# A hybrid encoder layer on one Trainium2 core: four small changes to the start, the first projection, the seam behind it, and the end

## The chip, the cores and the metric

The kernel runs on one core of one Trainium2 chip. The time is the device time of one execution in microseconds (us); the figure given is the median of three runs. A profiled execution of the same program gives the trace and the page of the profile. Of the engines, TensorE (PE) multiplies matrices, with weight loads (PEld) that overlap the products; VectorE (DVE), ScalarE (ACT) and GpSimd (POOL) work on vectors; SyncE (SP) only issues transfers (DMAs), which ScalarE and GpSimd can issue as well.

## The reference, cut to what matters

One layer for 512 tokens of width 2048, all in float32:

```python
def rmsnorm(x, w):
    return x * lax.rsqrt(jnp.mean(x * x, axis=-1, keepdims=True) + NORM_EPS) * w

h = rmsnorm(x, attn_norm_w)
aq, ak, av, gq, gk, gv, gr, glr = split(h @ w_in)
attn = mixture_of_dilations(heads(aq), heads(ak), heads(av), rel_bias_table)  # three windowed patterns
gla_out = ...                       # gated linear attention in both directions, from gq, gk, gv, gr, glr
x = x + concatenate([attn, gla_out]) @ w_out
h = rmsnorm(x, ffn_norm_w)
x = x + (silu(h @ w_gate) * (h @ w_up)) @ w_down     # hidden width 5632
return rmsnorm(x, final_norm_w)
```

The change touches four places of this computation: the first norm's factors at the very start, the projection to `aq` and `ak`, the passage from it to the next projection, and the last rows of the final norm.

## The kernel before, in words

**Precision.** Each float32 operand of a product is split in two: a rounded high part (a cast, mostly on ScalarE) and the remainder (a subtraction on VectorE). A product is then three matmuls: high by high, high by low, low by high.

**Buffers.** SBUF buffers come from lists that are first in, first out: `get` takes the front of the list, `put` appends at its back. `s2` holds buffers of 128x512 (named a in the profile), `s4` buffers of 128x1024 and larger groups (b). A buffer that has been put back early may be taken again at once; the instruction that writes it then waits until its last reader, a DMA too, is done. `ps` are the eight PSUM banks.

**Stages, in order.** (1) The start: `start0` issues the loads of x's first blocks and of the first weights, the norm's weights (`wrow1`, 16x128) are turned into columns with a transpose (L1154) that needs the identity `idn`, and `prep(0)` transposes x's first block (L450), scales it (L455) and so makes the first operand of the first matmul (L346). `spin(n)` issues n matmuls on a buffer of zeros (L1124) that fill TensorE's time. (2) A projection to `av`. (3) The first projection proper, class `Front`: the columns of `aq` and `ak` in 8 units of 256 columns with four pieces of the contraction each. (4) The other projections of `w_in`, run as jobs over a stream of weights `st`; the attention and the gated linear attention run beside them as side work. (5) The product with `w_out`. (6) The gate and up products of the feed-forward layer, class `Feed`: 44 units, of which 42 use the same emptying code as `Front`. (7) The product with `w_down`, and `finish`, which makes the final norm.

**Units of the first projection and of the feed-forward layer.** Their products use sums of blocks (L1399, L1401 add weights; L1412 casts; L1417 subtracts), so that seven products in seven banks replace eight. `products` issues one piece: 28 wide matmuls (L1508) and 28 narrow ones (L1494). After a unit's last piece `evac7` empties the seven banks into five `s2` buffers `t, v, r1, r2, r3` and one `s4` buffer `c`: ScalarE copies (L1534 into `t`, L1535 to L1542 into `r3, r2, r1, c`), VectorE adds and subtracts (lambdas in L1528 and L1529). A `yield` later, VectorE adds `v` to `c`, and GpSimd issues four DMAs that add `r1`, `r2` and twice `r3` into `c` (L1554 to L1557; `b<-a` in the trace). VectorE then scales `c` and it is stored. In `before` the two buffers `t, v` are put back first, and `r1, r2, r3` after the DMAs are issued. In the stage of `Front` the list then holds just these five.

**The stream and the seam.** `st.split(upto)` casts half pieces (L237, ScalarE) and subtracts (L218, VectorE) up to a number, and gives raw buffers back for the next loads. The seam is where the last unit of `Front` ends and the next job begins, with matmul L337; that job's first `split` stands, in program order, behind the last unit's `evac7`.

**The end.** `finish` works through four row blocks of 128 tokens. For the last block and its last 512 columns `last(ys)` forms the products in two halves of 256 columns (L2059), adds them to the residual (L2073), takes the sum of squares with ScalarE (`Square` with a sum), multiplies by the norm's weights (L2078), forms the reciprocal root with `Ln`, `Exp` and one Newton step in small operations (L2081 to L2085 and the lines behind them), scales the four pieces of 512 columns (L2092) and stores them.

The order of the instructions on each engine is that of the program. Engines run on their own and wait for one another through semaphores.

Of the kernel before, what the change touches and what calls it, by code (L numbers as in the profile page):

```python
# [18 lines left out]
AF = mybir.ActivationFunctionType  # L19
OP = mybir.AluOpType  # L20
# [3 lines left out]
P = 128  # L24
D = 2048
# [6 lines left out]
EPS = 1e-6  # L32
# [86 lines left out]
def layer(nc, tc, x, attn_norm_w, w_in, rel_table, gw_f, gb_f, gw_b, gb_b, gla_norm_w, w_out,  # L119
# [7 lines left out]
    with tc.manual_schedule(), \  # L127
# [302 lines left out]

        dve.memset(warm, 0.0)
        xt[0] = [s4.get(F32, [P, 4, 256]) for _ in range(2)]
        act.dma_start(out=wrow1, in_=attn_norm_w[0].rearrange("(r c) -> r c", c=P))
        act.dma_start(out=idn, in_=c_idn)

        rb = {}
        hT = {}
# [74 lines left out]
        def squares(c, t, tiles, ss):  # L512
            junk = s2.get()
            act.activation(junk.t, tiles[t].t, AF.Square, accum_out=ss[:, t * 4 + c:t * 4 + c + 1])
            put(junk)

        sum1, rstd1 = small[:, 16:20], small[:, 20:24]
# [609 lines left out]
        def start0():  # L1127
            tables(EXP_LN)
            spin(5)
            for k in range(4):  # L1130
                first_x(k)
                if k % 2 == 0:
                    pc = st.pieces[k // 2]
                    pc[1] = s4.get()
                    st.held += 1
                    st.n_dma += 1
                for src, dst in pc[0]:
                    sp.dma_start(out=dst(pc[1].t)[:, k % 2:k % 2 + 1], in_=src[:, k % 2:k % 2 + 1])
            for c in range(1, 4):
                xt[c] = [s2.get() for _ in range(4)]  # L1140
            load_x(1, 0, 256)
            st.limit = 3
            st.load()
            load_x(1, 256, 512)
            st.limit = 4
            st.load()
            load_x(2, 0, 512)
            load_x(3, 0, 512)
            for r, w in ((0, ffn_norm_w), (16, gla_norm_w), (24, gb_f), (28, gb_b)):
                n = w[0].shape[0] // P  # L1150
# [3 lines left out]
            pe.transpose(b.t, wrow1, idn[0:16, 0:16])  # L1154
            dve.tensor_copy(wcol[:, 0:16], b.t)
            put(b)
            spin(2)
            prep(0)
            spin(1)

        def between0(i, b):
            if i == 0 and b == 1:
# [260 lines left out]
        class Feed(Blocks):  # L1423
# [100 lines left out]
            def evac7(self, u, banks):  # L1524
# [111 lines left out]
        class Front(Feed):  # L1636
# [24 lines left out]
            def run(self):  # L1661
                banks = {}
                for i, (u, q) in enumerate(self.seq):
# [371 lines left out]
        def finish():  # L2035
# [25 lines left out]
            def last(ys):  # L2061

                t, c = 3, 3
                m, r = scr[0][:, 0:1], scr[1][:, 0:1]
                pre, q = scr[0][:, 1:2], scr[1][:, 1:2]
                sm, sq = sum2[:, t:t + 1], scr[0][:, 2:3]
                junk = s2.get()
                x_ = x1[c][t].t
                for h in range(2):
# [3 lines left out]
                    dve.scalar_tensor_tensor(x_[:, cols], b.t[:, cols], rstd2[:, t:t + 1], x_[:, cols],  # L2073
                                             op0=OP.mult, op1=OP.add)
# [3 lines left out]
                    dve.tensor_tensor(ys[c].t[:, cols], x_[:, cols], wf[c].t[:, cols], op=OP.mult)  # L2078
                    if h == 0:
                        dve.tensor_reduce(sm, ss2[:, 4 * t:4 * t + 4], op=OP.add, axis=mybir.AxisListType.X)  # L2080
                        dve.tensor_scalar(pre, sm, 1.0 / D, EPS, op0=OP.mult, op1=OP.add)  # L2081
                act.activation(q, sq, AF.Ln, scale=1.0 / D, bias=pre)
                act.activation(r, q, AF.Exp, scale=-0.5)
                dve.scalar_tensor_tensor(m, sq, 1.0 / D, pre, op0=OP.mult, op1=OP.add)
                dve.scalar_tensor_tensor(q, r, r, m, op0=OP.mult, op1=OP.mult)  # L2085
                dve.tensor_scalar(q, q, -0.5, 1.5, op0=OP.mult, op1=OP.add)
                rs = rstdf[:, t:t + 1]
                dve.tensor_tensor(rs, r, q, op=OP.mult)
                act.activation(ys[2].t, ys[2].t, AF.Copy, scale=rs)
                for c in (0, 2, 1, 3):  # L2090
                    if c != 2:
                        dve.tensor_scalar(ys[c].t, ys[c].t, rs, None, op0=OP.mult)  # L2092
                    (act if c >= 2 else sp).dma_start(out=out[t * P:(t + 1) * P, c * 512:(c + 1) * 512], in_=ys[c].t)
                put(junk)

            def run():
                for t in range(4):
                    ys = []
                    for c in range(4):
# [8 lines left out]
                        squares(c, t, x1[c], ss2)  # L2108
# [54 lines left out]
```

## Time and profile before

| | |
|---|---|
| median of three runs | 2183.57 us (2182.68 to 2184.25) |
| profiled execution, its time | 2181.53 us |
| its span | 2179.8 us |
| TensorE busy | 2161.3 us, 99%, 12618 matmuls |
| weight loads busy | 1904.2 us, 87% |
| VectorE busy | 1771.2 us, 81% |
| ScalarE busy | 1195.9 us, 55% |
| GpSimd busy | 338.9 us, 16% |
| moved by DMA | 397.81 MB, mean 183 GB/s |
| chain that ended last | PE 89%, issue 6%, DMA 2%, DVE 2%, ACT 1% |

The span goes from the first to the last instruction that the profile shows; the profiled execution's own time is 1.7 us longer. Matmuls are pipelined and their ends are modelled, so a busy TensorE isn't always one at its pace. In a row of the timeline the columns are the start, the duration, engine, line, operation, out<-in, shapes, count, and in brackets the idle time before it and what ended it. A row of the chain of waits has the start, the duration and what ran; a row of the waits has what waited, for what, the sum of the time in us, how often, and the longest. A row of the windows has, behind the length, for each of PE, PEld, DVE, ACT and POOL the busy time and count (PE's sum first), then the granted clock (1.00 is full), the share of DMA time and GB/s.

### The profile page before, as it was taken

What the parts mean: (1) busy time and instruction counts of PE and PEld (TensorE: products, weight loads), DVE (VectorE), ACT (ScalarE), POOL (GpSimd) and SP (SyncE); (2) the same over time, 40 slices, a digit from 0 to 9 for tenths busy, and PEclk for the clock granted to TensorE, in tenths of its full rate; (3) what the DMA queues carried; (4) which work ended last, traced back from release to release, by engine and by line L of the source; (5) the groups of instructions that cost most, each with busy time, mean ns of one, the idle gap of its engine ahead of it and who ended that gap; (6) DMA issues with size and microseconds to landing.
All of it is one profiled execution on the core that took longest, in us unless ns stands there. A gap on an engine that the chain in (4) does not pass through costs nothing.

```text
span 2179.8 us, 34563 instructions
## 1 busy us (share of the span) xinstructions
PE 2161.3 (99%) x12618; PEld 1904.2 (87%) x12618; DVE 1771.2 (81%) x3073; ACT 1195.9 (55%) x2189; POOL 338.9 (16%) x474
## 2 busy tenths in 40 slices
PE   9999999999999999999999999999999999999998
PEld 7888878888888888988888888888888899999986
DVE  5698767776766557899999898998999888898885
ACT  7445456776554335555555555555555655555562
POOL 0011231110011110012212122121221220021300
PEclk9999999999999999999999999999999999999999
DMA  6376774543337873377767777677776975576982
GB/s 201 125 187 173 189 226 141 176 140 111 105 103 270 288 247 107 120 182 177 198 176 183 180 176 196 178 181 182 177 196 176 263 201 182 181 183 157 283 304 78
DMA packets 256856, 397.81 MB, mean 183 GB/s; under 512 B 18925, under 2 KB 154269, under 8 KB 256686
## 3 DMA queue, kind: packets, MB, share of 16 engines
q1 hardware_dynamic: 201262, 272.43, 39.3%
q0 software_dynamic: 54960, 122.58, 24.9%
q8 instruction: 99, 1.62, 0.3%
q14 instruction: 71, 0.58, 0.1%
q10 hardware_dynamic: 464, 0.60, 0.1%
HBM read 285.37 MB, written 64.29 MB: 160 GB/s over the span
## 4 chain that ended last, share of the span: by engine, by line
PE 89%; issue 6%; DMA 2%; DVE 2%; ACT 1%; POOL 0%; ACTq 0%; DVEq 0%; POOLq 0%
PE ps L1508 27%; PE ps L1494 14%; PE ps L346 6%; PE ps L347 6%; PE ps L348 6%; PE ps L1864 5%; PE ps L1865 5%; PE ps L1863 5%; PE ps L339 3%; PE ps L337 3%; PE ps L338 3%; DMA b<-a 2%; PE ps L662 1%; PE ps L1086 1%; PE ps L630 1%
## 5 line engine op out<-in xcount | busy, mean ns | idle before, releaser
L1412 ACT CAST b<-b 128x768 fp32r<-128x768 f32 (+1 forms) x537 | 489.4, 945 | 338.5 <-DVE b L1417 151.2
L1417 DVE TENSOR_TENSOR b<-b,b 128x768 fp32r<-128x768 f32 (+1 forms) x537 | 563.6, 1084 | 32.9 <-ACT b L1412 21.5
L1508 PE MATMUL ps<-b,b 128*128 128x512 f32 x1552 | 451.4, 393 | 0.4 <-ACT b L1412 0.2
L1508 PE MATMUL ps<-a,b 128*128 128x512 f32 x1248 | 366.0, 394 | 3.3 <-DVE b L1528 3.3
L1508 PEld LDWEIGHTS ps<-b,b 128*128 128x128 f32 x1552 | 263.5, 188 | 30.6 <-ACT b L1412 0.7
L1494 PEld LDWEIGHTS ps<-b,b 128*128 128x128 f32 x1552 | 253.1, 190 | 35.8
L1494 PE MATMUL ps<-b,b 128*128 128x256 f32 x1552 | 275.6, 280 | 0.0
L1494 PEld LDWEIGHTS ps<-a,b 128*128 128x128 f32 x1248 | 208.1, 189 | 34.1 <-DVE b L1417 0.5
L1508 PEld LDWEIGHTS ps<-a,b 128*128 128x128 f32 x1248 | 207.2, 189 | 23.3 <-ACT a L1540 4.0
L1494 PE MATMUL ps<-a,b 128*128 128x256 f32 x1248 | 223.8, 281 | 0.0
L1399 DVE TENSOR_TENSOR b<-b 128x512 f32<-128x512 f32 x244 | 167.2, 685 | 17.8 <-DMA b<-in_w_down_dram 7.0
L1864 PE MATMUL ps<-b,b 128*128 128x256 f32 x624 | 176.8, 283 | 0.0
L1863 PE MATMUL ps<-b,b 128*128 128x256 f32 x624 | 176.8, 283 | 0.0
L1865 PE MATMUL ps<-b,b 128*128 128x256 f32 x624 | 176.8, 283 | 0.0
L346 PE MATMUL ps<-b,b 128*128 128x512 f32 x352 | 139.8, 397 | 0.3 <-ACT b L455 0.3
L348 PE MATMUL ps<-b,b 128*128 128x512 f32 x352 | 137.6, 391 | 0.0
L347 PE MATMUL ps<-b,b 128*128 128x512 f32 x352 | 137.5, 391 | 0.0
L1865 PEld LDWEIGHTS ps<-b,b 128*128 128x128 f32 x624 | 119.9, 192 | 0.0
L1863 PEld LDWEIGHTS ps<-b,b 128*128 128x128 f32 x624 | 119.9, 192 | 0.0
L1864 PEld LDWEIGHTS ps<-b,b 128*128 128x128 f32 x624 | 119.9, 192 | 0.0
L218 DVE TENSOR_TENSOR b<-b,b 128x512 fp32r<-128x512 f32 x143 | 95.9, 686 | 26.1 <-ACT b L237 26.0
L1401 DVE TENSOR_TENSOR b<-b,b 128x256 f32<-128x256 f32 x244 | 103.8, 425 | 8.4
(296 smaller groups left out, 4351.7 us busy)
## 6 DMA issues: line engine op xcount, KB each, us to landing
b<-in_w_gate_dram SPq DMA_DIRECT2D x109, 512.0 KB, 3.9
b<-in_w_up_dram SPq DMA_DIRECT2D x88, 512.0 KB, 3.7
b<-in_w_down_dram SPq DMA_DIRECT2D x88, 512.0 KB, 5.9
b<-in_w_in_dram SPq DMA_DIRECT2D x78, 512.0 KB, 4.0
b<-a POOLq DMA_DIRECT2D x150, 256.0 KB, 4.6
b<-in_w_out_dram SPq DMA_DIRECT2D x32, 512.0 KB, 6.6
gd<-b POOLq DMA_DIRECT2D x22, 512.0 KB, 3.9
b<-gd SPq DMA_DIRECT2D x22, 512.0 KB, 5.6
```

The source lines that it names most:

```text
L346: mm(o, xh.t[:, c], wh.t[:, w], start=first and not on, stop=False, skip_group_check=on)
L347: mm(o, xh.t[:, c], wl.t[:, w], start=False, stop=False, skip_group_check=on)
L348: mm(o, xl.t[:, c], wh.t[:, w], start=False, stop=last, skip_group_check=on)
L1399: dve.tensor_tensor(s_[:, :, 0:2], r[:, :, 1:3], r[:, :, 0:1].to_broadcast(shape), op=OP.add)
L1401: dve.tensor_tensor(s_[:, :, 3], s_[:, :, 2], r[:, :, 3], op=OP.add)
L1412: act.copy(o, src)
L1417: dve.tensor_tensor(o, src, h, op=OP.subtract)
L1494: mm(o, wl, xh, start=False, stop=end, skip_group_check=True)
L1508: mm(o.rearrange("p (s t) -> p s t", s=2), wh, x_, start=first and p == 0, stop=False, skip_group_check=True)
L1863: mm(o, xh[:, t], wh, start=first and h == 0, stop=False, skip_group_check=True)
L1864: mm(o, xh[:, t], wl, start=False, stop=False, skip_group_check=True)
L1865: mm(o, xl[:, t], wh, start=False, stop=last, skip_group_check=True)
```

## The change

1. The load of the identity goes to SP's queue, ahead of all its other loads, instead of being second on ScalarE's queue. Of the filling matmuls, one stands before `prep(0)` and two behind it, instead of the reverse.
2. In `evac7`, the five buffers are put back together after the DMAs are issued, in the order `r1, r3, t, r2, v`, instead of `t, v` before and `r1, r2, r3` after.
3. In `Front.run`, before the products of the last piece of the last unit, two half pieces of the next job's weights are split.
4. At the end, for the last block: the sums of squares of its first four groups go to `ss1`, together with a constant for the epsilon that GpSimd writes. ScalarE adds up these five columns, scaled, with a copy. The last 256 columns' squares are summed by VectorE (`tensor_tensor_reduce`) instead of ScalarE. The product of root and correction is no longer formed; VectorE scales all four pieces by both factors, and the stores alternate between the queues of SP and ScalarE.

```diff
         xt[0] = [s4.get(F32, [P, 4, 256]) for _ in range(2)]
+        sp.dma_start(out=idn, in_=c_idn)
         act.dma_start(out=wrow1, in_=attn_norm_w[0].rearrange("(r c) -> r c", c=P))
-        act.dma_start(out=idn, in_=c_idn)
...
+            spin(1)
+            prep(0)
             spin(2)
-            prep(0)
-            spin(1)
...
                 add(c[:, 256:768], c[:, 256:768], v.t)
-                put(t, v)
                 pool.dma_start(out=c[:, 0:512], in_=r1.t, accum_op=OP.add)
                 pool.dma_start(out=c[:, 512:1024], in_=r2.t, accum_op=OP.add)
                 pool.dma_start(out=c[:, 256:768], in_=r3.t, accum_op=OP.add)
                 pool.dma_start(out=c[:, 768:1024], in_=r3.t[:, z], accum_op=OP.add)
-                put(r1, r2, r3)
+                put(r1, r3, t, r2, v)
...
+                    if u == len(self.units) - 1 and q == 3:
+                        st.split(jobs[n_front].first + 2)
                     self.products(i, banks[u])
...
         def load_wf():
+            pool.memset(ss1[:, 4:5], EPS * D)
...
-                    acc = (ss2[:, 4 * t + 3:4 * t + 4], sq)[h]
-                    act.activation(junk.t[:, cols], x_[:, cols], AF.Square, accum_out=acc)
+                    if h == 0:
+                        act.activation(junk.t[:, cols], x_[:, cols], AF.Square, accum_out=ss1[:, 3:4])
+                        act.activation(ss1[:, 8:13], ss1[:, 0:5], AF.Copy, scale=1.0 / D, accum_out=total)
+                        dve.tensor_tensor(ys[c].t[:, cols], x_[:, cols], wf[c].t[:, cols], op=OP.mult)
+                        continue
+                    dve.tensor_tensor_reduce(junk.t[:, cols], x_[:, cols], x_[:, cols], 1.0 / D, 0.0,
+                                             op0=OP.mult, op1=OP.add, accum_out=sq)
+                    act.activation(q, sq, AF.Ln, bias=total)
+                    act.activation(r, q, AF.Exp, scale=-0.5)
+                    dve.tensor_tensor(m, sq, total, op=OP.add)
                     dve.tensor_tensor(ys[c].t[:, cols], x_[:, cols], wf[c].t[:, cols], op=OP.mult)
-                    if h == 0:
-                        dve.tensor_reduce(sm, ss2[:, 4 * t:4 * t + 4], op=OP.add, axis=mybir.AxisListType.X)
-                        dve.tensor_scalar(pre, sm, 1.0 / D, EPS, op0=OP.mult, op1=OP.add)
-                act.activation(q, sq, AF.Ln, scale=1.0 / D, bias=pre)
-                act.activation(r, q, AF.Exp, scale=-0.5)
-                dve.scalar_tensor_tensor(m, sq, 1.0 / D, pre, op0=OP.mult, op1=OP.add)
-                dve.scalar_tensor_tensor(q, r, r, m, op0=OP.mult, op1=OP.mult)
+                dve.scalar_tensor_tensor(q, r, m, r, op0=OP.mult, op1=OP.mult)
                 dve.tensor_scalar(q, q, -0.5, 1.5, op0=OP.mult, op1=OP.add)
-                rs = rstdf[:, t:t + 1]
-                dve.tensor_tensor(rs, r, q, op=OP.mult)
-                act.activation(ys[2].t, ys[2].t, AF.Copy, scale=rs)
-                for c in (0, 2, 1, 3):
-                    if c != 2:
-                        dve.tensor_scalar(ys[c].t, ys[c].t, rs, None, op0=OP.mult)
-                    (act if c >= 2 else sp).dma_start(out=out[t * P:(t + 1) * P, c * 512:(c + 1) * 512], in_=ys[c].t)
+                for c in range(4):
+                    o = ys[c].t
+                    dve.tensor_scalar(o, o, r, q, op0=OP.mult, op1=OP.mult)
+                    (sp, act)[c % 2].dma_start(out=out[t * P:(t + 1) * P, c * 512:(c + 1) * 512], in_=o)
```

More of the change, by code (lines that the diff above doesn't have):

```diff
@@ L510, in squares1, with squares @@
             put(junk)
-        def squares(c, t, tiles, ss):
+        def squares(c, t, tiles, ss, at_=None):
             junk = s2.get()
-            act.activation(junk.t, tiles[t].t, AF.Square, accum_out=ss[:, t * 4 + c:t * 4 + c + 1])
+            m = c + (4 * t if at_ is None else at_)
+            act.activation(junk.t, tiles[t].t, AF.Square, accum_out=ss[:, m:m + 1])
             put(junk)
@@ L2063, in last @@
                 t, c = 3, 3
-                m, r = scr[0][:, 0:1], scr[1][:, 0:1]
-                pre, q = scr[0][:, 1:2], scr[1][:, 1:2]
-                sm, sq = sum2[:, t:t + 1], scr[0][:, 2:3]
+                sq, total = ss1[:, 16:17], ss1[:, 17:18]
+                m, r, q = ss1[:, 18:19], ss1[:, 19:20], ss1[:, 15:16]
                 junk = s2.get()
@@ L2107, in run @@
                         residual(c, t, b)
-                        squares(c, t, x1[c], ss2)
+                        squares(c, t, x1[c], ss2 if t < 3 else ss1[:, 0:4], 0 if t == 3 else 4 * t)
                         if t == 3:
```

## The prediction

> **What bounds the kernel now.** I read first the waits of TensorE over the whole execution, then the busy time by stretch.
>
> ```profile
> PE ps L1508 <- DVE b L1528: 3.5, 5, 1.7
> PE ps L1154 <- DMA idn<-in_c_idn_dram: 1.3, 1, 1.3
> PE ps L337 <- ACT b L237: 1.3, 1, 1.3
> ```
> ```profile
> 20.00:105.00 85.00, 85.00 (x397) 69.01 (x396) 55.19 (x118) 54.44 (x130) 2.79 (x5) 1.00 0.41 135
> 920.00:1720.00 800.00, 800.00 (x4592) 702.64 (x4591) 728.89 (x1128) 440.48 (x742) 155.07 (x184) 1.00 0.72 185
> ```
>
> TensorE is busy 85.00 us of 85 and 800.00 of 800 (first figure behind the stretch's length). So it is the bound, and a gain exists only where it waits or before it starts and after it ends. The three waits are the places that the change aims at; whatever is won there stays won, because nothing idles behind it.
>
> **Part 1, the copies' buffers.** The first projection has units of 28 matmuls a piece and four pieces. At the end of a unit ScalarE and VectorE empty its banks into t, v, r1, r2, r3. The view is ScalarE's timeline; L1534 (into t) marks the end of a unit, L1535 is the first copy into r3.
>
> ```profile
> 161.24 0.37 ACT L1534 COPY a<-ps 128x256 f32<-128x256 f32 x1 [0.54 <-PE ps L1494]
> ...
> 180.74 0.37 ACT L1534 COPY a<-ps 128x256 f32<-128x256 f32 x1
> 185.21 0.37 ACT L1535 COPY a<-ps 128x256 f32<-128x256 f32 x1 [4.10 <-DMA b<-a]
> ...
> 200.76 0.37 ACT L1534 COPY a<-ps 128x256 f32<-128x256 f32 x1
> ...
> 262.96 0.37 ACT L1534 COPY a<-ps 128x256 f32<-128x256 f32 x1 [4.60 <-PE ps L1494]
> ```
>
> An undisturbed unit takes 180.74 - 161.24 = 19.50 us. The next four marks should lie at 78.00 more, and the last one lies at 82.22: TensorE loses 4.2 us here, more than the idle column says, because that counts only time between modelled ends. VectorE and the chain of waits show the round that causes it:
>
> ```profile
> 183.71 0.88 DVE L1529 TENSOR_TENSOR a<-a,ps 128x256 f32<-128x256 f32 x2
> 185.89 0.42 DVE L1528 TENSOR_TENSOR a<-ps,a 128x256 f32<-128x256 f32 x1 [1.31 <-ACT a L1536]
> ```
> ```profile
> 193.32 6.07 DMA b<-a
> ...
> 201.72 3.70 DMA b<-a
> ...
> 213.63 6.38 DMA b<-a
> ...
> 223.04 3.80 DMA b<-a
> ```
> ```profile
> 187.26 0.47 PE L1508 MATMUL ps<-a,b 128*128 128x512 f32 x1 [0.29 <-DVE b L1528]
> ```
>
> Before: VectorE writes v at 185.89; 7.43 later, at 193.32, the first pair of accumulating DMAs goes out; 8.40 later the last one, which reads r3; it lands 3.70 later, at 205.42. The copy into r3 has waited for that, because t, v, r1, r2, r3 come back to the same five buffers each time. From landing to the next v are 0.10 (landing 185.11 by the same rows, copy 185.21) and 0.68 (185.21 to 185.89). A round is 0.78 + 7.43 + 8.40 + 3.70 = 20.31, 0.81 more than 19.50. The banks must be free when v starts by mark + 4.63 (the unit of 180.74 had v 5.15 after its mark and its next mark came 200.76 - 180.74 = 20.02 later, 0.52 lost).
>
> After: `put(r1, r3, t, r2, v)` gives the next unit t in old r1, v in old r3, r1 in old t, r3 in old v. The build's order shows two sets alternating. Now ScalarE's copies wait only for the matmuls, and the landing is awaited by VectorE's write of v itself, at landing + 0.10. Queued behind that wait on VectorE are the sums of the banks and the low parts of the next pieces; they stood behind the same landing before, 0.68 later. A round becomes 19.63. VectorE is free for v from 183.71 + 0.88 = 184.59, mark + 3.85, so there is a reserve of 4.63 - 3.85 = 0.78. Three rounds at 0.13 over and one slow one (213.63 to 223.04 is 9.41, 1.01 more than 8.40; with the landing's 0.10 more 1.24 over) are 1.63; less the reserve about 0.8 is still lost. Gain 4.2 - 0.8 = 3.4; with no slow round 4.2; with two or three slow rounds 2.4. The copy into t waits for old r1's DMA, landed at 193.32 + 6.07 = 199.39, before the mark at 200.76: it costs nothing, and up to 1 us a unit if that DMA takes 7.4. In the feed-forward stage the same line runs for 42 units; there the ring holds more than ten buffers, and one comes round after two units or more, long after its DMA (a rival below says what if not).
>
> **Part 2, the seam.** Two halves of the next job's first weights are rounded (L237 on ScalarE, L218 on VectorE) before the last piece's products instead of behind the last unit's copies.
>
> ```profile
> 266.71 0.39 PE L1494 MATMUL ps<-b,b 128*128 128x256 f32 x2
> 268.35 0.50 PE L337 MATMUL ps<-b,b 128*128 128x512 f32 x1 [1.25 <-ACT b L237]
> ```
> ```profile
> 256.32 4.29 DVE L1417 TENSOR_TENSOR b<-b,b 128x768 fp32r<-128x768 f32 x4
> 263.36 0.42 DVE L1528 TENSOR_TENSOR a<-a,ps 128x256 f32<-128x256 f32 x1 [2.75 <-ACT a L1534]
> ```
>
> The two L1494 follow each other within 0.12 (0.39 for two of 0.28), so L337 could start at 266.95: 1.40 lost. ScalarE sat idle for 4.60 us before 262.96 (row above), VectorE 2.75 before 263.36: two casts and two subtractions fit in, and their queue behind them (the copies, the banks' sums) is not late. The raw piece was loaded a unit earlier. The first bank is a free one and the next come from sums that start at 263.36. Gain 1.4; 1.0 if a bank becomes the next late thing, 1.8 if the three short-fed matmuls behind 268.35 also go at pace.
>
> **Part 3, the start.** The identity goes first on SP's queue instead of second on ScalarE's, everything of SP's goes one issue later, and two of the four filling matmuls move behind the first transposes. The chain of waits at the start, and the filler before it:
>
> ```profile
> 1.23 3.48 DMA idn<-in_c_idn_dram
> ...
> 4.84 0.26 PE ps L1154
> 5.10 1.15 PE ps L1124 x4
> 6.26 0.87 PE ps L450 x4
> ...
> 7.15 0.70 ACT b L455
> ...
> 7.88 0.80 PE ps L346
> ```
> ```profile
> 1.06 2.50 PE L1124 MATMUL ps<-warm 128*128 128x128 f32 x10 [1.06 <-DVE warm L431]
> 0.74 0.43 SPq L423 DMA_DIRECT2D b<-in_x_dram  x1
> ```
> ```profile
> wrow<-in_attn_norm_w_dram ACTq DMA_DIRECT2D x1, 8.0 KB, 2.4
> GB/s 0 0 0 0 0 0 0 0 125 153 171 296 328 326 369 355 371 294 275 284 294 326 337 325 305 285 325 330 373 398 364 328 330 335 355 357 325 376 360 353
> ```
>
> Issued at 0.74, the identity lands between 0.74 + 2.4 (another first transfer's time) and 0.74 + 3.48 (its own): 3.1 to 4.2. I take 3.3, nearer to the first transfer, since nothing is in front of it. The filler ends at 3.56, so L1154 starts at 3.6; 0.26, half the filler 0.58, the transposes 0.87, four filling matmuls 1.15 (longer than the 0.70 of L455 beside them): L346 at about 6.5. Gain 1.4; with a landing at 4.2 0.7. It needs x's first block by 4.4 and the first weights by 5.5. Their issues move by about 0.49 (0.43 and the gap to the next at 1.23). The rates (40 slices of 0.225 us) add up to 478 KB by 3.6 us, against 584 KB for the first four transfers, so both should be there by 3.6 + 0.3 + 0.5 = 4.4. If they are later, the gain goes to 0, at worst to -0.5. The window of 20 to 105 us shows that the work behind is then paced by TensorE.
>
> **Part 4, the end.**
>
> ```profile
> 2169.84 0.28 PE L2059 MATMUL ps<-b,b 128*128 128x256 f32 x1
> ```
> ```profile
> 2170.36 0.15 DVE L2081 TENSOR_SCALAR small<-small 128x1 f32<-128x1 f32 x1
> 2170.43 0.47 DVE L2073 SCALAR_TENSOR_TENSOR a<-ps,small,a 128x256 f32<-128x256 f32 x1
> 2170.94 0.42 DVE L2078 TENSOR_TENSOR a<-a,a 128x256 f32<-128x256 f32 x1
> 2171.48 0.16 DVE L2084 SCALAR_TENSOR_TENSOR small<-small 128x1 f32<-128x1 f32 x1
> 2172.04 0.22 DVE L2085 SCALAR_TENSOR_TENSOR small<-small 128x1 f32<-128x1 f32 x1 [0.40 <-ACT small L2083]
> ...
> 2172.68 0.48 DVE L2092 TENSOR_SCALAR a<-a,small 128x512 f32<-128x512 f32 x1
> ```
> ```profile
> L640 DVE CUSTOM_DVE_ANT_0 a<-ps,b 128x512 f32<-128x512 f32 x64 | 43.6, 682 | 3.4 <-PE ps L631 3.2
> L640 DVE DVE_READ_ACCUMULATOR2_ANT small<- 128x1 f32 x64 | 5.3, 83 | 0.0
> ```
>
> The last products end at 2170.12, but L2073 starts at 2170.43, behind two small operations that go to ScalarE: 0.28 won. The sum of squares, 0.54 on ScalarE (2170.94 to 2171.48), becomes VectorE's multiply with a sum, which this kernel has as L640: 0.68 + 0.08 at 512 columns, at 256 about 0.42 (as L2078) + 0.08: 0.04 won. Of the 0.64 from L2085 to the first scaling one small operation of 0.19 goes: 0.5 in all. Four scalings on VectorE instead of three and one on ScalarE are hidden as long as the stores behind are slower. If the scaling with two factors loses the speed of L2092, 0.27 goes back (512 columns at L2073's step against 0.48): 0.1 to 0.55.
>
> [...]
>
> **Sum.** 3.4 + 1.4 + 1.4 + 0.5 = 6.7 us. The profiled execution took 2181.53 us (span 2179.8), so 2174.8; the median of the runs shown lies 2.04 above it, at 2183.57: 2176.9 us. With all parts at their low ends (2.4, 1.0, 0.3, 0.1) it is 2179.8, with all at the high ones (4.2, 1.8, 1.7, 0.55) 2175.3. 0.2% is 4.4 us, about what a measurement of this kernel can tell from no change; the line is at 2179.2.
>
> **The rivals.**
> (a) The wait only changes engines: the accumulations, started earlier, collide with weight loads, every round is as slow as the one of 213.63, and the first projection gains 0.5. For it: the DMAs take 12 of 20 us in the round. Against it: three of four rounds had 8.4 or less with the same loads. 6.7 - 2.9 = 3.8: 2179.8, no change that can be told.
> (b) The start does not pay, x's first block being the late one: 6.7 - 1.4 - 0.5 = 4.8: 2178.8.
> (c) The matmuls also come to full pace earlier. The transposes take 0.87 for four at 6.26 where two 128x512 matmuls at 266.71 and later are spaced 0.23; with the idle 1.28 us before L1154 gone, the slow phase would end sooner, for some 0.7 more: 2176.2. [...]
> (d) Slower: in the feed-forward stage a rotated buffer is still being read by its DMA when VectorE wants v. VectorE is busy 728.89 of 800 us, 41 units, so it has 1.7 us a unit to spare; a wait longer than that by x costs 42x. It outweighs the other parts above x = 0.27 (11.1 us), and at x = 0.4 gives 2183.57 + 16.8 - 6.7 = 2193.7. Against it: a buffer comes round after two units, 39 us, and a round's DMAs end within 20.
>
> **How the numbers follow.** Forecast 0.58, (a) 0.15, (b) 0.07, (c) 0.14, (d) 0.06. Faster by over 0.2%: forecast, (b), (c), 0.79; within: (a), 0.15; slower: (d), 0.06. The range goes from 2174.2 (under (c), with part 1 at its best) to 2181.2 (past (a), with the start at its worst), and leaves out (d) and the tails.
>
> **What would show it.** Right: marks of the first projection 19.5 to 19.8 us apart; ScalarE's copy into r3 with no wait for a DMA and VectorE's first v waiting for one; L337 following without idle time; L1154 near 3.6 and L346 near 6.5; the first scaling about 2.5 us after the last product's start in place of 2.84. Wrong: marks over 20.3 apart; TensorE idle in the feed-forward stage; a wait of L450 for x.

## The result, and the profile after

The changed kernel takes 2174.13 us (median of six runs, 2173.06 to 2175.53), the kernel before 2182.78 in six runs. The ratio is 0.9961 with a 95% interval of 0.9948 to 0.9974: 0.39% faster, 8.65 us by the medians. The span of the profiled execution went from 2179.8 to 2172.0, 7.8 us less (its own time is 2173.79). Forecast were 6.7 us and 2176.9, worked out from the 2183.57 of the first three runs.

The first view again is TensorE's waits (what waited, for what, us in total, times, longest). All rows of the changed kernel:

```profile
PE ps L1125 <- DVE warm L431: 1.1, 1, 1.1
PE ps L631 <- DVE b L677: 0.8, 1, 0.8
PE ps L1866 <- DVE b L1418: 0.6, 1, 0.6
PE ps L1509 <- DVE b L1529: 0.4, 2, 0.2
PE ps L339 <- DVE a L218: 0.3, 1, 0.3
PE ps L1509 <- ACT b L1413: 0.2, 1, 0.2
```

The three waits that the change aimed at are gone, or down from 3.5 to 0.4 (line numbers moved by one or two: L1508 is L1509 now). The third row is new: L1866, the first products with w_down, waits 0.6 for VectorE. More on it below.

Where the time went can be read by setting matmul n of one trace beside matmul n of the other, since their order is the same. The start of matmul n is earlier by 1.62 us at the first L346, 2.42 at the first unit's mark, 6.03 at the last unit's mark, 7.44 at L337, 7.82 four matmuls later, and 7.25 at the last matmul of all; the span ends 7.8 earlier. So: start 2.4, first projection 3.6, seam 1.4 and 0.4 behind it, minus 0.57 on the way from there to the last matmul (0.53 of it at the new wait), end 0.5.

### The profile page after: what moved, and what is told of

It is laid out like the page before. It is cut to its first block, busy times and chain, and to the rows that moved or that the text cites. A ratio compares the mean times of both kernels' runs of the same rounds, so it can differ in the third digit from the quotient of the medians.

```text
span 2172.0 us, 34569 instructions
## 1 busy us (share of the span) xinstructions
PE 2159.5 (99%) x12618; PEld 1902.2 (88%) x12618; DVE 1771.5 (82%) x3073; ACT 1197.1 (55%) x2188; POOL 339.6 (16%) x475
## 3 DMA queue, kind: packets, MB, share of 16 engines
q8 instruction: 99, 1.62, 0.3%
## 4 chain that ended last, share of the span: by engine, by line
PE 95%; DVE 2%; DMA 1%; issue 1%; ACT 0%; POOL 0%; DVEq 0%; ACTq 0%; POOLq 0%
PE ps L1509 28%; PE ps L1495 14%; PE ps L346 6%; PE ps L348 6%; PE ps L347 6%; PE ps L1866 5%; PE ps L1867 5%; PE ps L1865 5%; PE ps L339 3%; PE ps L337 3%; PE ps L338 3%; PE ps L663 1%; DMA b<-a 1%; PE ps L1087 1%; PE ps L631 1%
## 5 line engine op out<-in xcount | busy, mean ns | idle before, releaser
L1418 DVE TENSOR_TENSOR b<-b,b 128x768 fp32r<-128x768 f32 (+1 forms) x537 | 563.8, 1084 | 33.2 <-ACT b L1413 21.2
L1509 PE MATMUL ps<-b,b 128*128 128x512 f32 x1552 | 451.0, 393 | 0.4 <-ACT b L1413 0.2
L1509 PE MATMUL ps<-a,b 128*128 128x512 f32 x1248 | 365.6, 394 | 0.2 <-DVE b L1529 0.2
L1509 PEld LDWEIGHTS ps<-b,b 128*128 128x128 f32 x1552 | 263.5, 188 | 30.7 <-ACT b L1413 0.7
L1509 PEld LDWEIGHTS ps<-a,b 128*128 128x128 f32 x1248 | 207.3, 189 | 19.9 <-issue 0.5
L1866 PE MATMUL ps<-b,b 128*128 128x256 f32 x624 | 176.6, 283 | 0.0
L346 PE MATMUL ps<-b,b 128*128 128x512 f32 x352 | 139.4, 396 | 0.0
L348 PE MATMUL ps<-b,b 128*128 128x512 f32 x352 | 137.4, 390 | 0.0
L347 PE MATMUL ps<-b,b 128*128 128x512 f32 x352 | 137.2, 390 | 0.0
L1866 PEld LDWEIGHTS ps<-b,b 128*128 128x128 f32 x624 | 119.8, 192 | 0.0
```

What stands on the lines that cost most here:

```text
L346: mm(o, xh.t[:, c], wh.t[:, w], start=first and not on, stop=False, skip_group_check=on)
L347: mm(o, xh.t[:, c], wl.t[:, w], start=False, stop=False, skip_group_check=on)
L348: mm(o, xl.t[:, c], wh.t[:, w], start=False, stop=last, skip_group_check=on)
L1418: dve.tensor_tensor(o, src, h, op=OP.subtract)
L1509: mm(o.rearrange("p (s t) -> p s t", s=2), wh, x_, start=first and p == 0, stop=False, skip_group_check=True)
L1866: mm(o, xh[:, t], wl, start=False, stop=False, skip_group_check=True)
```

## The experiments

All ten kernels beside the two, by the same points of their traces. "First L346" is where the real work starts; "to mark 1" is the time from there to the first unit's copy into t; "lost" is the time between the first and the eighth mark over 7 x 19.50 = 136.50; "seam" is from the eighth mark to L337; "tail" from the start of the last matmul to the end of the span. All in us. Ratios are to runs of the kernel before on the same chip, with their 95% intervals. Where the text below gives a landing of a transfer or a time from which the full clock was granted, it is from the semaphore and clock records kept in the traces, which the views shown here don't print.

| kernel | median | ratio | first L346 | to mark 1 | lost | seam | tail |
|---|---|---|---|---|---|---|---|
| before | 2182.78 | | 7.88 | 114.35 | 4.22 | 5.39 | 9.91 |
| changed | 2174.13 | 0.9961 [0.9948, 0.9974] | 6.26 | 113.56 | 0.61 | 3.98 | 9.38 |
| p_order | 2178.67 | 0.9984 [0.9975, 0.9992] | 8.00 | 114.89 | 0.42 | 5.39 | 9.88 |
| p_seam | 2180.03 | 0.9989 [0.9979, 0.9998] | 8.34 | 114.40 | 3.21 | 3.98 | 9.95 |
| p_start | 2179.20 | 0.9984 [0.9975, 0.9993] | 6.13 | 113.56 | 4.41 | 5.39 | 9.81 |
| p_end | 2180.39 | 0.9992 [0.9983, 1.0001] | 7.98 | 114.70 | 4.57 | 5.39 | 9.03 |
| m_early | 2227.44 | 1.0206 [1.0192, 1.0220] | 7.88 | 114.16 | 50.62 | 5.99 | 9.50 |
| m_early2 | 2178.69 | 0.9980 [0.9971, 0.9989] | 7.95 | 114.74 | 0.00 | 5.40 | 9.87 |
| m_fill | 2180.47 | 0.9993 [0.9984, 1.0002] | 7.40 | 113.61 | 3.02 | 5.40 | 9.92 |
| m_nofill | 2175.22 | 0.9968 [0.9956, 0.9981] | 6.38 | 114.57 | 0.39 | 3.98 | 9.37 |
| m_best | 2226.24 | 1.0198 [1.0184, 1.0212] | 6.51 | 115.82 | 51.01 | 3.98 | 8.91 |
| m_best2 | 2173.08 | 0.9957 [0.9944, 0.9971] | 6.13 | 113.76 | 0.00 | 3.98 | 9.01 |

The seam's column shows how exact a trace can be here: 5.4 or 3.98, nothing between, with 5.99 in m_early alone. The medians can tell p_order, p_seam and p_start from no change, p_end not; for that one the traces have to do.

**Each part by itself.** p_order is the kernel before with the order of the buffers alone:

```diff
-                put(t, v)
...
-                put(r1, r2, r3)
+                put(r1, r3, t, r2, v)
```

> The kernel before with part 1 alone (the five buffers put back after the DMAs in the order r1, r3, t, r2, v). Theory (a loop from VectorE's v through the accumulating DMAs back to v, 0.68 shorter, against a unit of 19.50): the marks of the first projection lie 19.5 to 19.9 us apart, the last of them 3.4 to 3.7 us earlier against the first than before, the time 3.4 to 3.7 us (0.16%) less. The wait of L337 for L237 stays at about 1.3. Rival 1 (the changed order also delays the last stores of the feed-forward stage): TensorE then waits about 0.6 us for VectorE's subtractions as the product with w_down begins, as in the trace of after, and the net gain is 3.0. Rival 2 (the gain in the first projection came from the start's shift against the DMAs and not from the order): the marks stay over 20.2 apart and nothing is won.

The first projection loses 0.42 in place of 4.22, as the first theory has it, and the wait of L337 stays (seam 5.39). ScalarE's timeline of p_order, the copies into t and r3 (L1534, L1535) of one unit, and the copy into t of the next:

```profile
220.39 0.37 ACT L1534 COPY a<-ps 128x256 f32<-128x256 f32 x1 [0.95 <-PE ps L1494]
221.78 0.37 ACT L1535 COPY a<-ps 128x256 f32<-128x256 f32 x1 [1.02 <-PE ps L1494]
239.89 0.37 ACT L1534 COPY a<-ps 128x256 f32<-128x256 f32 x1 [0.49 <-PE ps L1494]
```

The copy into r3 comes 1.39 behind the mark, here and in the seven other units, and waits for the matmuls; before it came 4.47 behind (180.74 to 185.21) and waited for the DMA. TensorE has no wait at the beginning of the product with w_down in this trace, so rival 1 falls. Rival 2 falls with the marks.

p_seam splits two halves of the next job's weights before the last products:

```diff
+                    if u == len(self.units) - 1 and q == 3:
+                        st.split(jobs[n_front].first + 2)
                     self.products(i, banks[u])
```

> The kernel before with part 3 of the change alone (two halves of the next job's weights split before the last piece's products). Theory: L337 follows the last L1494 at 0.24 without a wait; 1.4 to 1.7 us less in the trace (1.4 of the wait and 0.26 of the second and third matmul behind it, which were fed late). Rival (part of the seam's gain in the trace of after was the first projection's): 1.0 or less.

The seam is 1.41 shorter, and four matmuls later the trace is another 0.38 ahead. That is the theory, with a little more behind L337 than its 0.26.

p_start is the start alone:

```diff
+        sp.dma_start(out=idn, in_=c_idn)
         act.dma_start(out=wrow1, in_=attn_norm_w[0].rearrange("(r c) -> r c", c=P))
-        act.dma_start(out=idn, in_=c_idn)
...
+            spin(1)
+            prep(0)
             spin(2)
-            prep(0)
-            spin(1)
```

> The kernel before with the start alone (identity first on SP's queue, one filler before and two behind the first transposes). Theory (the idle time before L1154 goes, and TensorE comes to its full pace a fixed time of about 5.4 us after it last began to work without a pause): L346 at 6.3 instead of 7.9 and the matmuls behind at 0.23 apart from about 7.8; 2.4 us less at matmul 30 and in the time. Rival (only the idle time goes): 1.4 to 1.6 us less. The first projection still loses about 4 us.

The first L346 comes at 6.13, 1.75 us sooner than in the trace of before, and the way from there to the first mark is 0.79 shorter: 2.5 in all, the theory's 2.4 and not the rival's 1.4 to 1.6. The end of the loop in the first projection is untouched (4.41 lost), and TensorE's waits show it, with something else:

```profile
PE ps L1508 <- DVE b L1528: 3.5, 4, 2.1
PE ps L1864 <- DVE b L1417: 1.3, 1, 1.3
```

L1864, where w_down begins, waits 1.3 in a kernel that has neither the new order nor the new end. So this wait is not made by the order of the buffers. It is 0 in before, p_order, m_fill, m_best and m_best2, 0.2 in p_seam and p_end, 0.6 in the changed kernel and m_early, 0.7 in m_nofill, and 1.2 in m_early2, which has no part of the change. VectorE stands behind a store there, as its timelines show (the changed kernel, then p_start):

```profile
1760.50 0.69 DVE L1400 TENSOR_TENSOR b<-b 128x512 f32<-128x512 f32 x1 [2.45 <-DMA gd<-b]
```
```profile
1766.69 0.69 DVE L1399 TENSOR_TENSOR b<-b 128x512 f32<-128x512 f32 x1 [3.96 <-DMA gd<-b]
```

When that store lands differs from one trace to the next; why is open.

p_end has the end alone, the fourth part of the diff.

> The kernel before with the end alone. Theory: from the start of the last matmul to the span's end 9.4 us instead of 10.0, that is 0.5 to 0.6 less in the trace, which no median can tell from no change (within 0.1%). Rival (the gain at the end in the trace of after was the stores' scatter): no difference in the span's tail over 0.2.

The tail is 9.03, against 9.81 to 9.95 in before, p_order, p_seam and p_start, so 0.8 to 0.9; with the changed kernel's 9.38 the gain is 0.4 to 0.6 (m_early, with the old end too, has 9.50). The records of the landings sort this out. From the start of the last matmul to the first scaling it is 2.37 in each kernel with the new end and 2.83 or 2.84 in each with the old one, 0.47 less. The first store is issued 0.41 earlier, but the last one 0.16 later; even so the last store lands at 7.39 to 7.41 in the five traces with the new end and at 7.90 to 7.94 in the seven with the old one. The four stores land 0.6 to 0.8 apart, so it seems to be the start of the first one that counts. This steady 0.5 is the gain; the 1.5 to 2.0 us from the last landing to the end of the span differ from trace to trace under either end (1.62 in p_end, 1.98 in the changed kernel, 1.59 in m_early, 1.98 in before), and are the scatter of the tail's column.

**What the start's gain is made of.** m_fill keeps the identity where it was and only fills TensorE's time until it lands:

```diff
-            spin(5)
+            spin(9)
```

> The kernel before with nine filling matmuls at the start instead of five; the identity lands as before, so nothing can start sooner. Theory (full pace comes a fixed time after TensorE's last pause, about 5.4 us): with the pause of 1.3 to 1.7 us filled, TensorE works without one from 1.06, the first L346 is at 7.9 to 8.5 as before, or later by the overshoot of up to 0.3, but the ten matmuls behind it take 2.0 us in place of 2.8, and the trace gains 0.5 to 0.8 against a trace of before with the same landing of the identity. Rival (the slow matmuls belong to the first operands and not to the pause): the ten take 2.8 as before, and nothing is won or 0.2 is lost.

The identity lands no earlier (4.70, before 4.71), and yet the first mark comes at 121.00, where the six other traces with the old start have it at 122.0 to 122.9. TensorE's timeline of m_fill (an x4 or x18 row takes in that many matmuls):

```profile
1.06 4.21 PE L1124 MATMUL ps<-warm 128*128 128x128 f32 x18 [1.06 <-DVE warm L431]
5.20 0.28 PE L1154 MATMUL ps<-idn,wrow 16*128 16x16 f32 x1
6.02 0.60 PE L450 MATMUL ps<-idn,b 128*128 128x128 f32 x4
7.40 0.50 PE L346 MATMUL ps<-b,b 128*128 128x512 f32 x1 [0.56 <-ACT b L455]
8.52 0.60 PE L450 MATMUL ps<-idn,b 128*128 128x128 f32 x4
```

The transposes L450 take 0.60 for four at 6.02; in the trace of before they took 0.87 on the chain at 6.26 and still 0.85 at 9.53. So the matmuls' own pace has doubled by 6.02, while before it doubled at about 10.3 (L347 and L348 start 0.43 apart at 8.48, and from 10.47 on L346 to L348 follow each other within 0.24). The clock records agree: full clock from 5.57 in m_fill, from 10.28 in before. The 0.56 of idle time at 7.40 did not set it back: the L347 behind it, at 7.74, took 0.40, where the one at 8.48 in before took 0.63. The saving is 1.2 us against the trace of before, more than expected, because the transposes and with them L346 come sooner as well. m_nofill is the opposite, the changed kernel without the two matmuls behind the first transposes:

```diff
             prep(0)
-            spin(2)
```

> The changed kernel without the two filling matmuls behind the first transposes. Theory (a pause of 0.7 us just before the first real matmul sets TensorE's slow phase back): L346 still at 6.2, then ten matmuls in 2.8 or more in place of 2.0, and slow ones until about 11; 1 us or more lost. Rival (only pauses of over a us count, or none): the same marks as the changed kernel within 0.2, and the fillers do nothing.

The theory holds: L346 is at 6.38, but the way to the first mark is 114.57 instead of 113.56, 1.0 us lost. Its timeline:

```profile
6.38 0.80 PE L346 MATMUL ps<-b,b 128*128 128x512 f32 x1 [0.78 <-DVE b L473]
7.83 1.05 PE L450 MATMUL ps<-idn,b 128*128 128x128 f32 x4
9.44 0.39 PE L348 MATMUL ps<-b,b 128*128 128x512 f32 x1
```

The full clock is granted from 9.31 here and from 6.43 in the changed kernel. So here a pause of 0.78 before the pace had doubled cost 1.0; one of 0.56 after it had, in m_fill, cost nothing that the way to the first mark shows (113.61, 113.56 in the changed kernel). Each of the two kernels was traced once, but all twelve traces sort the same way: the four with no longer pause before the pace had doubled (changed, p_start, m_best2, m_fill) have 113.56 to 113.76 to the first mark, the eight others 114.16 to 115.82.

**Whether it is the loop's length.** In the first projection the four DMAs can be issued sooner instead of rotating the buffers. m_early moved the sum with v and the DMAs ahead of the yield:

```diff
                 put(*banks)
-                yield
+                if self is ff:
+                    yield
                 add(c[:, 256:768], c[:, 256:768], v.t)
...
                 put(r1, r2, r3)
+                if self is not ff:
+                    yield
```

> The kernel before (its order of buffers too), but in the first projection VectorE's sum with v and the four accumulating DMAs stand ahead of the yield, directly behind the other sums of evac7. Theory (what costs the 4.2 us is the length of the loop, and not which buffer goes where): the 7.4 us between v and the first DMA become about 2.2, the loop 0.8 + 2.2 + 8.4 + 3.7 = 15.1 us, under a unit's 19.50; all marks of the first projection 19.5 us apart though the copy into r3 still follows the old r3, 4 us or more less than before in the trace, as much as the new order brings. Rival 1 (the copies must be free of the DMAs): marks over 20. Rival 2 (the sum of 0.6 us ahead of the next pieces' sums makes VectorE late): TensorE waits for L1417's operands in each unit, up to 0.6 a unit, and half of the gain goes. L337 still waits 1.3 for L237.

It lost 45 us, and by none of the three mechanisms named. TensorE's waits stand where rival 2 puts them, but are of another size and cause; the views are a row of these waits, then GpSimd's and VectorE's timelines of m_early:

```profile
PE ps L1494 <- DVE b L1417: 34.2, 12, 6.5
```
```profile
153.72 1.21 POOL L1558 DMA_DIRECT2D b<-a  x1
154.26 1.22 POOL L1655 DMA_DIRECT2D qkd<-b  x1
```
```profile
160.53 0.69 DVE L1399 TENSOR_TENSOR b<-b 128x512 f32<-128x512 f32 x1 [9.06 <-DMA qkd<-b]
```

The store of the unit before (L1655, L1652 in before) is issued at the end of a unit, and the DMAs of the new unit now stand ahead of it on GpSimd's queue: the store goes out only behind both pairs, lands at 160.5, and VectorE, which takes the freed buffer for the next sums, stands still for 9.06. TensorE's waits make 34.2 of the 50.6 lost; behind the pauses its clock was halved too (two L1508 took 0.85 at 195.57 and 0.47 at 197.96), for five stretches of 6.83 us and one of 10.24 in this stage (the window of 190 to 220 us has a granted clock of 0.85). This is the collision with a queue that a moved step brings, not an answer on the loop. m_early2 keeps the scaling and the store first and moves the sum and the DMAs by one group of sums only:

```diff
                         next(done)
                     run_urgent()
                     if done:
+                        next(done)
                         urgent.append(done)
...
-                for _ in range(3 if u < len(self.units) - 2 else 7):
+                for _ in range((3 if u < len(self.units) - 2 else 7) + (self is not ff)):
```

> The kernel before, its order of buffers and all else kept, with the sum with v and the four accumulating DMAs moved ahead by one group of the next pieces' sums, but still behind the scaling and the store of the unit before on VectorE and on GpSimd's queue (which the first try of this had moved behind the DMAs). Theory (the length of the loop sets the marks, whichever buffer goes where): 3.5 us shorter, 16.8 us in place of 20.3, under 19.50; all marks of the first projection 19.5 us apart, the 4.2 us (3.7 to 5.3 in the traces so far) gone, though the copy into r3 still waits for the old r3 where that is late. Rival (the copies must be free of the DMAs, as in the changed kernel): steps of 20 and more from the fourth on.

All seven steps are 19.50 and nothing is lost, with the old order of buffers. (Its expectation gives 3.7 to 5.3 as the loss so far; by the table it is 3.0 to 4.6.) One copy into r3 still waits for its DMA (ScalarE's timeline of m_early2; behind it GpSimd's, where the first DMA follows the store by 0.92 instead of 4.45):

```profile
203.86 0.37 ACT L1535 COPY a<-ps 128x256 f32<-128x256 f32 x1 [2.79 <-DMA b<-a]
```
```profile
187.92 0.56 POOL L1652 DMA_DIRECT2D qkd<-b  x1 [10.31 <-DVE b L1651]
188.84 0.86 POOL L1554 DMA_DIRECT2D b<-a  x1 [0.35 <-DVE b L1399]
```

So it is the loop's length against the unit's 19.50 that counts, not which buffer goes where; the new order is one way to shorten it, and by the working of the prediction it took 0.68 off, where the earlier issue took 3.5 (4.45 less 0.92).

**Better versions.** m_best added the first form of the early DMAs to the changed kernel, and another start: the identity first and the norm's weights second on ScalarE's queue, x's first block first on SP's, and the transpose of the norm's weights behind those of x. The early DMAs and the lines taken out at the old place of that transpose, one filling matmul among them, are not shown again here.

```diff
-        sp.dma_start(out=idn, in_=c_idn)
+        act.dma_start(out=idn, in_=c_idn)
         act.dma_start(out=wrow1, in_=attn_norm_w[0].rearrange("(r c) -> r c", c=P))
...
             for t in range(4):
                 pe.transpose(b.t[:, t * P:(t + 1) * P], x_block(k, t), idn)
+            if k == 0:
+                bw = ps.get(F32, [P, 16])
+                pe.transpose(bw.t, wrow1, idn[0:16, 0:16])
+                dve.tensor_copy(wcol[:, 0:16], bw.t)
+                put(bw)
```

> The changed kernel with two more steps: the early sum and DMAs in the first projection as in m_early, and at the start the identity first on ScalarE's queue and the norm's weights second, SP's queue as in the kernel before, the transposes of x's first block ahead of that of the norm's weights. Theory: marks all 19.5 us apart (0.4 to 0.6 us less than the changed kernel), x's first block landing at about 3.7 instead of 4.33 and L346 at about 5.8 instead of 6.26; 1.0 less in the trace than the changed kernel's, 2173. Rival (the norm's weights, second on their queue, land after 5.3 and hold up L455): L346 later than 6.3 and the start loses what the marks win.

The 51 us are those of m_early. The start can be read for itself, in TensorE's timeline:

```profile
4.22 1.09 PE L450 MATMUL ps<-idn,b 128*128 128x128 f32 x4 [0.66 <-DMA b<-in_x_dram]
6.51 0.80 PE L346 MATMUL ps<-b,b 128*128 128x512 f32 x1
```

x's first block lands at 4.09, hardly before the changed kernel's 4.33, though it was issued first. L346 comes 0.25 later than in the changed kernel, and the full clock is granted only from 11.85, so the first mark is 2.5 later. Neither the theory nor the rival had that cost. The pause of 0.66 before L450 is the difference that the trace shows; that it alone puts the clock off so far is not shown (more on it in the last section). m_best2 is the changed kernel with the edit of m_early2:

> The changed kernel with the same move of the sum and the DMAs. Theory: all marks 19.50 apart, 0.4 to 0.6 us less than the changed kernel in the trace, everything else as there, so a median of 2173 to 2174 us. Rival (the 0.6 us of the sum ahead of the next pieces' sums makes these late, since VectorE is busy nine tenths of the unit): TensorE waits for L1418's operands and the kernel is no faster than the changed one, or slower by up to 4 us.

Steps of 19.50 throughout, 0.61 less lost than in the changed kernel, and a median of 2173.08, 1.05 under it. The two ratios, 0.9957 [0.9944, 0.9971] and 0.9961 [0.9948, 0.9974], overlap; that it is faster rests on the trace. VectorE is not late: TensorE has no wait for L1418.

## Why the prediction was right, and where its steps were off

**Part 1, the copies' buffers: forecast 3.4, measured 3.6** (4.22 less 0.61). ScalarE's and VectorE's timelines and the chain of waits of the changed kernel show the loop as the prediction put it together:

```profile
197.82 0.37 ACT L1535 COPY a<-ps 128x256 f32<-128x256 f32 x1 [0.65 <-PE ps L1495]
199.21 0.37 ACT L1536 COPY a<-ps 128x256 f32<-128x256 f32 x1 [1.02 <-PE ps L1495]
217.32 0.37 ACT L1535 COPY a<-ps 128x256 f32<-128x256 f32 x1 [1.02 <-PE ps L1495]
237.22 0.37 ACT L1535 COPY a<-ps 128x256 f32<-128x256 f32 x1
256.93 0.37 ACT L1535 COPY a<-ps 128x256 f32<-128x256 f32 x1 [3.52 <-PE ps L1495]
```
```profile
182.24 0.76 DVE L1529 TENSOR_TENSOR a<-ps,a 128x256 f32<-128x256 f32 x2 [0.84 <-PE ps L1509]
222.36 0.76 DVE L1529 TENSOR_TENSOR a<-ps,a 128x256 f32<-128x256 f32 x2 [2.30 <-ACT a L1543]
```
```profile
208.79 5.03 DMA b<-a
218.45 3.69 DMA b<-a
```

The copy into r3 (L1536 now) waits for no DMA. Up to the sixth mark the steps are 19.50. Then comes one slow round, 9.66 from the first pair of DMAs to the last: it lands at 218.45 + 3.69 = 222.14, and v is written at 222.36. The row puts the wait of 2.30 down to ScalarE's L1543, which ended at the same time; but v doesn't read what L1543 writes, and at 201.35 it was written before that unit's L1543 was done (202.65). The landing ended the wait, as the prediction had it. So it was in the rounds before, though the row at 182.24 names a matmul: the last DMAs landed at 182.12 and 201.23, and v was written at 182.24 and 201.35. From landing to landing the rounds are 19.84, 19.11, 20.91 and 19.82, where 19.63 and, for the slow one, 20.74 were expected. v is 5.04 behind its mark; over the 4.63 at which the banks must be free that makes 0.41, and the next step is 0.40 too long (217.32 to 237.22). The one after has 0.21. So 0.61 was lost where 0.8 were expected, with one slow round, as assumed: the unit before it had v 3.53 behind its mark, a reserve of 1.10 and not 0.78. Before-type orders lost 3.0 to 4.6 in five traces, the new order 0.4 to 0.6 in three.

**Part 2, the seam: forecast 1.4, measured 1.41, and 0.38 behind it**, 1.8 in all. This is the upper end of the 1.0 to 1.8 given, and its condition came true: the matmuls behind L337 go at pace too. L337 follows the last products without a pause:

```profile
260.69 0.39 PE L1495 MATMUL ps<-b,b 128*128 128x256 f32 x2
260.92 0.40 PE L337 MATMUL ps<-b,b 128*128 128x512 f32 x1
```

**Part 3, the start: forecast 1.4, measured 2.4**, outside its own -0.5 to 1.7. The step that failed is that the sum ended at L346. Up to there it held: L1154 at 3.6 and L346 at 6.5 were forecast, and TensorE's timeline has

```profile
3.49 0.28 PE L1155 MATMUL ps<-idn,wrow 16*128 16x16 f32 x1
4.37 1.12 PE L450 MATMUL ps<-idn,b 128*128 128x128 f32 x4
6.26 0.56 PE L346 MATMUL ps<-b,b 128*128 128x512 f32 x1
8.53 0.40 PE L346 MATMUL ps<-b,b 128*128 128x512 f32 x1
```

What the sum left out is rival (c): the matmuls behind L346 come to full pace sooner, priced at 0.7, an estimate of the author's with no working of its own, and measured at 0.79 (114.35 less 113.56). It was given a chance of 0.14 as something beside the forecast; m_fill and m_nofill show that it goes with the pause, so it belonged in the sum: the trace of before had the slow transposes and the pause beside each other. The filling matmuls behind the first transposes, costed as filler of 1.15 us, are worth 1.0 by themselves (m_nofill). The pair of traces was kind to the old start, besides: four others of it have the first mark 0.4 to 0.7 later, one 0.2 earlier. (The row at 266.71 that rival (c) compares with is of 128x256 matmuls, 0.12 apart; 0.23 is the step of 128x512 ones, as before shows behind 10.47.)

The identity landed at 2.73, under the 3.1 to 4.2 of the working; L1155 came at 3.49 all the same, behind the ten filling matmuls, as the sum had it. Rival (b), x's block late, was near: the block landed at 4.33, where 3.61 was the time before and 4.4 was allowed, and the weight load of L450 waited 0.16 for it. The first weights landed at 5.11, later than the 4.4 worked out and before the 5.5 needed.

**Part 4, the end: forecast 0.5, measured 0.53**, and the same 0.53 to the last store's landing (7.93 and 7.40). VectorE's timeline of the changed kernel:

```profile
2163.43 0.42 DVE L2083 CUSTOM_DVE_ANT_0 a<-a 128x256 f32<-128x256 f32 x1
2163.78 0.08 DVE L2083 DVE_READ_ACCUMULATOR2_ANT ss<- 128x1 f32 x1
2164.96 1.91 DVE L2093 TENSOR_SCALAR a<-a,ss 128x512 f32<-128x512 f32 x4
```

The multiply with a sum takes 0.42 and 0.08, as worked out from L2078 and L640, with both sources the same buffer of SBUF. The four scalings are hidden behind the stores, as the prediction assumed: the last one starts 3.74 behind the last matmul's start, before 3.64, and the last store lands sooner all the same. The scaling by two factors takes 0.48 each (1.91 for four), as by one.

**The rivals.** (a) falls with the marks. (d) falls with the feed-forward stage: set matmul by matmul beside before, the changed kernel is 7.66 to 7.80 ahead all through it, and p_order 2.70 to 2.72. TensorE's window there is as full as before (VectorE 713.95, 714.08 before):

```profile
920.00:1700.00 780.00, 780.00 (x4482) 684.73 (x4481) 713.95 (x1101) 430.76 (x723) 151.78 (x180) 1.00 0.72 183
```

**Not in the prediction at all**: the 0.53 lost at the start of the product with w_down. It comes and goes from trace to trace, up to 1.3, and stands in kernels with no part of the change.

The sum: 2.42 + 3.61 + 1.41 + 0.38 - 0.57 + 0.53 = 7.8, the span's difference. So the four parts brought 8.35 where 6.7 were forecast, most of the difference in the start, and a loss that nobody had looked for took 0.57 back; that the total comes as near as it does is in part luck. What came is not the main forecast but rival (c), with more in it.

The time of 2174.13 lies 0.07 under the range's low end, 2174.2. That end does not come out of the prediction's own figures (under (c) with part 1 at its best they give 2176.2 - 0.8 = 2175.4; nor does the high end, since (a) with the start at its worst is 2181.7). The before of six runs, 2182.78, is 0.8 under the 2183.57 from which the prediction counted; as ratios to its own before, the range is 0.9957 to 0.9989, and the measured 0.9961 lies inside.

The single parts, by their traces, make 3.8 (p_order) + 1.8 + 2.5 + 0.5 = 8.6, near the 8.35, and by their medians 0.51% in place of 0.39%, each with an interval of some 0.09% to either side: so the parts add up, as far as these can tell.

## What to carry to other kernels

Where a ring of buffers closes through a DMA, add up the loop (copy, sum, issue, transfer, landing) and set it against the time of one turn of the bound engine: only the excess costs, and anything that takes it away, a rotated buffer or an earlier issue, brings about the same (3.8 and 4.2 us here, of 4.2). Before a step is moved ahead on one engine, list what then stands behind it on every queue that it uses; here the store behind four DMAs cost 45 us. At the start, keep the matrix engine busy without a pause until its matmuls run at full pace, and count the slow matmuls behind a pause as part of its price; here a pause of 0.78 made the way to the first mark 1.0 longer (m_nofill). At the end, count to the last landing of a store and not to its issue: here the last one was issued 0.16 later and landed 0.5 sooner.

## What was not expected of the hardware

**A pause while TensorE's matmuls were slow cost more than itself.** One of 0.78 made the way to the first mark 1.0 longer (m_nofill). With no pause over 0.2 us from 1.06 until then, the full clock was granted from 5.57 (m_fill), 6.43 (changed), 6.38 (p_start) and 7.33 (m_best2). With one of 1.3 or more that ended at 4.8 or later, and a shorter one before L346 (0.3 in the list of its waits), it came between 9.88 (m_early) and 11.55 (p_order), in before at 10.28; with one of 0.78 that ended at 6.38, at 9.31 (m_nofill). It is no fixed time behind the last long pause, as p_start's and m_fill's theories had it: 5.4 us in before, 6.6 in p_order, 2.9 in m_nofill. In three traces the changes of the clock lie whole multiples of 3.41 us apart: in m_early 153.60, 6.83, 20.48 and 10.24 (45, 2, 6 and 3 times), in before 2164.05 (634 times 3.4133) and in the changed kernel 2160.64 (633 times). Between traces of the same start the first change scatters by 1.7 us (9.88 to 11.55). m_best stands apart: from 4.22 its TensorE has only gaps of under 0.2, and the full clock comes at 11.85, 7.6 us later, where the four traces without a pause had it 4.5 to 6.3 us after 1.06. Why is open.

**The order of the first transfers said who waited.** The identity ahead of x's first block on the same queue, or ahead on another, put that block's landing off: 3.5 to 3.6 in the seven traces with the old start, 4.06 to 4.45 in the four with the new one, 4.09 in m_best. The last of the first four transfers (the norm's weights, the identity, x's block, the first weights) lands between 4.7 and 5.2 in all twelve, whatever the order.
